# An explicit order of steps between first stage and out-projection, a mask inside VectorE's maximum, and adaLN sums twice as wide

## The chip, the cores and the metric

The kernel runs on one core of one Trainium2 chip. The core's engines work side by side, each in its own order of instructions: TensorE (PE: matmuls; PEld: its weight loads), VectorE (DVE), ScalarE (ACT), GpSimd (POOL), and SyncE (SP), which issues most DMAs. They wait for one another by semaphores. The metric is the device time of one execution in microseconds, as the median of several runs.

## What is computed

One layer of a hybrid decoder on 512 tokens of width 1024, in f32:

```python
mod = silu(c) @ w_ada + b_ada                  # sh1, sc1, gt1, sh2, sc2, gt2
h = rmsnorm(x) * (1 + sc1) + sh1
z = h @ w_in                                   # HGRN2: hq hf hi hg; NSA: nq, 6 x kv, gates
o_hg = rmsnorm(hgrn2(hq, hf, hi)) * silu(hg)   # 4 heads of 128
o_nsa = g0 * compressed + g1 * selected + g2 * window    # 8 heads of 64, softmax each
x = x + gt1 * (concat(o_hg, o_nsa) @ w_out)
h2 = rmsnorm(x) * (1 + sc2) + sh2
a, v = split(causal_dwconv(h2 @ w_up))
x = x + gt2 * ((silu(a) * v) @ w_down)
```

With 512 tokens, 8 blocks of 64 and 16 to be selected, the selected branch is plain causal attention over all blocks, and the window of 512 also covers every earlier token. So both branches are causal attention with keys and values of their own.

## The kernel before

**Stages.** The tokens lie in four tiles of 128. Every f32 product of the projections is done as three matmuls of split operands (`mm3`, L143 to L146: high by high, high by low, low by high); `split` (L139) makes the parts, the high one by a cast on ACT (L140), the low one by a subtraction on DVE (L141). First come the adaLN sums for the first norm, the norm and the query and forget projections of the first stage (to about 60 us). Then, until 289 us, the section that the change concerns: the remaining input projections, HGRN2 and the attention, all mixed. Then the output projection (`oh`), the up-projection (`u`) to 590 us, and the down-projection (`dn`) to the end.

**The section's streams.** It is made of Python generators, each of which issues some instructions and yields:

- the dense chain: key/value projection (`kva`), a second one, the HGRN2 query, forget, value and gate projections (`pT`: six matmuls of 512 columns per step), the compression of blocks (`cmp_hidden`) and, at its end, the rest that comes ahead of the output projection (`late`);
- `prep`: norm and rotation of queries and keys. `hrs` is the reciprocal root (POOL, L367), `xr` the scaled row (DVE, L703), `dst` the rotated one (L710, L712), `qhl` its split; PE transposes that (L769, `ps`);
- `hg_levels(0)` and `hg_levels(1)`: HGRN2 by levels of doubling block length, with products `lev` on PE (L1138) and masks, decays and states (`hgA`, `hgQ`, `hgK`, `hgtot`, `hgS`) mostly on DVE;
- `ada_sums`: the adaLN products for the later stages, as sums on DVE over tiles of w_ada: `aacc = aw * cs + aacc` (L1287, the first of a row by L1289), 512 columns at a time;
- `attention`: one unit after another.

**An attention unit** is one head of one tile of queries. For tiles 0 and 1 it does both branches at once (n = 2); for tiles 2 and 3 each branch (b) is a unit of its own (n = 1), 32 in all; a further unit per tile is the compressed branch. A unit goes through stations that are staggered over the units: `scores` (two matmuls into a PSUM bank `S`, L984 and L985; a third with the identity adds the causal mask to the diagonal block, L986; DVE takes the negated maximum, L988), `expo` (ACT, L1005: exponential from `S` into `pt`, with the row sum), `weigh` (at every odd head, for the pair: reciprocal and gate on DVE, L1019 and L1020; then both heads' `pt` are scaled, by DVE for b = 0, L1027, by ACT for b = 1, L1025), `flip` (PE transposes `pt` into bank `F`, L1036; ACT copies it, L1043), and `values` (matmuls with `pT`). `LAG = 4`: a unit's flip is issued four units after its scores.

**What sets the order.** Each engine executes its instructions in the order in which the program issues them. `emit` mixes streams in proportion to a number given to each: the next step comes from the stream whose share done is smallest. The section is a series of such calls, with the shares AN, DN, L0N, L1N, KVN, AD0 to AD6 and ADN.

Of the kernel before, what the change touches and what calls it, by code (L numbers as in the profile page):

```python
# [39 lines left out]
FP1 = 4  # L40
FP3 = 6
LAG = 4
AN = 82
DN = 29
L1N = 40
L0N = 19
KVN = 16
PREP1 = ('sq2 sq3 rq2 rq3', '', 'nq0', 'fq0', 'nq1', '', 'lq0', 'fq1', 'nq2', '', 'lq1', 'fq2', 'nq3', 'lq2', 'fq3', 'lq3')
PREP2 = ('sk0 rk0 sk1 rk1', 'nk0 fk0 sk2 rk2', 'nk1 fk1 sk3 rk3', 'lk0 nk2 fk2')
PREP3 = ('lk1 nk3 fk3 sa0 ra0', 'sa1 ra1 lk2 na0 fa0', 'sa2 ra2 lk3 na1 fa1', 'sa3 ra3 la0 na2 fa2')  # L50
PREP4 = ('', 'la1 na3 fa3', '', 'la2', '', 'la3', '', '')
ROWS = (2, 3, 5)
COLS = (0, 0, 1, 1, 2, 1, 2, 2)
SUMS = {3: (4, 4, 4), 5: (6, 5, 3), 6: (7, 5, 3)}
# [2 lines left out]
VLAG = 1  # L57
ADL = 1
ADAS = (3, 4, 2)
ADW = 512  # L60
AD0, AD1, AD2, AD3, AD4, AD5, AD6 = 8, 4, 0, 0, 4, 4, 2
ADN = 26
LEVELS = (1, 2, 4, 8, 16, 32, 64)

C_IDENT = 0
# [34 lines left out]
def hybrid_layer_kernel(ctx: ExitStack, tc: tile.TileContext, d: dict, out: bass.AP, dbg=None):  # L100
# [21 lines left out]
    def PS(s="ps"):  # L122
        return psum.tile([P, 512], F32, tag="b", name=nm(s))

    def TMP(shape, dt=F32, tag="tmp"):
        n = 1
        for a in shape[1:]:
            n *= a
        if n > 256:
            return tp.tile(shape, dt, tag="t2", name=nm(tag), bufs=8)  # L130
        return tp.tile(shape, dt, tag="t1", name=nm(tag), bufs=4)

    def SM(shape, tag, dt=F32):
        return sm.tile(shape, dt, tag=tag, name=nm(tag))
# [13 lines left out]
    def dump(name, ap):  # L148
        if dbg is not None:
            o = nc.dram_tensor("dbg_" + name, ap.shape, F32, kind="ExternalOutput").ap()  # L150
            sp.dma_start(o, f32(ap))
            dbg.append(name)

    def emit(*streams):

        st = [[0, max(n, 1), g] for g, n in streams]
        while st:
            e = min(st, key=lambda e: e[0] / e[1])
            e[0] += 1
            try:  # L160
                next(e[2])
            except StopIteration:
                st.remove(e)

    def chain(*gens):
        for g in gens:
# [710 lines left out]
    def cmp_flat():  # L877
        ps = PS()
        pe.transpose(ps[:, 0:32], perow, ident[0:32, 0:32])
        ve.tensor_copy(pet, ps[:, 0:32])  # L880
        for b in range(2):
            f = G([16, 2, 32], s="flat")
            gp.memset(f[:, :, :, 31:32], 0.0)
            for g in range(2):
                for m2 in range(2):
                    src = kv2[:, b, g, 8 * m2:8 * m2 + 248].rearrange("p (n m) -> p m n", m=8)
                    (gp if g else ve).tensor_tensor(f[:, 8 * m2:8 * m2 + 8, g, 0:31], src,
                                                    pet[:, b * 16 + 8 * m2:b * 16 + 8 * m2 + 8].unsqueeze(2)
                                                    .to_broadcast([P, 8, 31]), ALU.add)
# [86 lines left out]
    def scores(u):  # L976
        i, h, bs = u
        if h is None:
            return cmp_scores(i)
        g, W, n = h // 4, (i + 1) * P, len(bs)  # L980
        ps = PS("S")
        o = ps[:, 0:n * W].rearrange("p (b j t) -> p j b t", b=n, t=P)
        bsl = slice(bs[0], bs[0] + n)
        pe.matmul(o, QS[i][:, h], KK[g, 0][:, 0:i + 1, bsl], start=True, stop=False)  # L984
        pe.matmul(o, QS[i][:, h], KK[g, 1][:, 0:i + 1, bsl], start=False, stop=False)  # L985
        pe.matmul(o[:, i], identb, causb.unsqueeze(1).to_broadcast([P, n, P]), start=False, stop=True)  # L986
        mx = SM([P, 2], "mx")
        ve.tensor_reduce(mx[:, 0:n], ps[:, 0:n * W].rearrange("p (b w) -> p b w", b=n), AX.X, ALU.max,  # L988
                         negate=True)
        return ps, mx  # L990

    def expo(u, st):
        i, h, bs = u
        if h is None:
            sc.activation(st, st, AF.Exp)
            return st
        ps, mx = st
        W, n = (i + 1) * P, len(bs)
        pt = TMP([P, 512], tag="pt")
        if h % 2 == 0:  # L1000
            sums[0] = SM([P, 2, 2], "su")
        su = sums[0]
        for e in range(n):
            sl = slice(e * W, (e + 1) * W)
            sc.activation(pt[:, sl], ps[:, sl], AF.Exp, bias=mx[:, e:e + 1], accum_out=su[:, h % 2, e:e + 1])  # L1005
        return pt, su

    def weigh(u, st):
        i, h, bs = u
        if h is None:  # L1010
            cmp_norm(i, st)
            return st
        if h % 2 == 0:
            first[0] = st[0]
            return st[0]
        pt, su = st
        W, n = (i + 1) * P, len(bs)
        gv = gates[:, i].rearrange("p (h b) -> p h b", b=3)
        ve.reciprocal(su[:, :, 0:n], su[:, :, 0:n])  # L1019
        ve.tensor_tensor(su[:, :, 0:n], su[:, :, 0:n], gv[:, h - 1:h + 1, 1 + bs[0]:1 + bs[0] + n], ALU.mult)  # L1020
        for a, p_ in enumerate((first[0], pt)):
            for e, b in enumerate(bs):
                sl = slice(e * W, (e + 1) * W)
                if b:
                    sc.activation(p_[:, sl], p_[:, sl], AF.Copy, scale=su[:, a, e:e + 1])  # L1025
                else:
                    ve.tensor_scalar(p_[:, sl], p_[:, sl], su[:, a, e:e + 1], None, ALU.mult)  # L1027
        return pt
# [251 lines left out]
    def ada_sums():  # L1280
        for n, (s, k) in enumerate(ada_rows):
            if k == 0:
                aacc[s] = G([D], s="aacc")
            for c in range(0, D, ADW):
                o, w = aacc[s][:, c:c + ADW], aws[n][:, c:c + ADW]
                if k:
                    ve.scalar_tensor_tensor(o, w, cs[:, k:k + 1], o, ALU.mult, ALU.add)  # L1287
                else:
                    ve.tensor_scalar(o, w, cs[:, 0:1], None, ALU.mult)  # L1289
                if c + ADW == D and k == KT - 1:  # L1290
                    summed.append(s)
                yield
                if c + ADW == D:
                    ada_load()
# [28 lines left out]
    def ada_out():  # L1323
        for s in ADAS:
# [72 lines left out]
    gt1 = G([D], s="gt1")  # L1397
    sp.dma_start(gt1, d["b_ada"][0, 2 * D:3 * D].partition_broadcast(P))
    adas = ada_out()
    adss = ada_sums()  # L1400

    def late():
        for _ in range(4):
# [4 lines left out]
    def part(g, n):  # L1408
        for _ in range(n):
            if next(g, g) is g:  # L1410
                return
            yield

    gp.tensor_copy(causb, cb[:, C_CAUS:C_CAUS + P])
    kv = proj_kv()
    for _ in prep(("sq0 sq1 rq0 rq1",)):
        pass
    for j in range(2):
        hg_forget(0, j, accf[j])
    for _ in range(2):  # L1420
        ada_load()
    emit((kv, KVN), (prep(PREP1), len(PREP1)), (part(adss, AD0), AD0))
    emit((proj_a(), 8), (prep(PREP2), len(PREP2)), (part(adss, AD1), AD1))
    attn = attention(adas)
    lev0 = hg_levels(0, As[0])
    lev1 = hg_levels(1, As[1])
    emit((proj_T(lambda j, a: hg_query(0, j, a)), 8), (prep(PREP3), len(PREP3)), (part(adss, AD2), AD2))
    emit((proj_T(lambda j, a: hg_forget(1, j, a)), 8), (prep(PREP4), len(PREP4)), (part(attn, 10), 10), (part(adss, AD3), AD3))
    cmp_flat()
    hq1 = proj_T(lambda j, a: hg_query(1, j, a))  # L1430
    hv0 = proj_tok(hg_value_out)
    emit((chain(part(hq1, 4), cmp_hidden(0), cmp_hidden(1), hq1), 12), (part(attn, 12), 12),
         (part(lev0, 10), 10), (part(adss, AD4), AD4))
    emit((chain(part(hv0, 4), cmp_hidden(2), cmp_hidden(3)), 8), (part(attn, 6), 6), (part(lev0, 6), 6), (part(adss, AD5), AD5))
    dense = chain(hv0, hg_value_odd(), proj_T(hg_gate_out(0)), proj_T(hg_gate_out(1), False), late())
    emit((cmp_out(), 4), (part(dense, 4), 4), (part(attn, 4), 4), (part(lev0, 4), 4), (part(adss, AD6), AD6))
    emit((attn, AN), (dense, DN), (lev0, L0N), (lev1, L1N), (adss, ADN))
    assert len(summed) == 3
    for _ in adas:
        pass  # L1440
# [251 lines left out]
```

## Time and profile before

| | |
|---|---|
| Median of three runs | 716.05 us (714.89 to 716.3) |
| The profiled execution | 714.7 us; its span 712.9 us |
| Granted TensorE clock, mean | 1.00 |
| Busy | PE 98%, DVE 65%, ACT 45%, POOL 15% |
| The section: first kv matmul to first matmul ahead of the output projection | 60.2 to 289.3 us |

The span runs from the first to the last recorded instruction. A row of the timeline has the start in us, the duration in us, engine, line, operation, output<-input and shapes, how many instructions it stands for, and in brackets how long the engine had been idle just before and what released it. A row of grouped instructions ends with count, busy time in us, mean of one in ns, and idle time before them with its releasers. Durations of neighbours can overlap, since an engine takes up the next instruction while the last one drains; the distance from start to start is then the better price of one.

### The profile page before, as it was taken

Reading aid. Unit: us, or ns where it says so; the run is one execution under the profiler, and the core shown is the slowest. Engines: PE = TensorE matmul, PEld = TensorE weight load, DVE = VectorE, ACT = ScalarE, POOL = GpSimd, SP = SyncE. Lnnn points to the kernel's source line nnn. Section 1 sums busy time; section 2 is a strip of 40 time slices with the busy share of each in tenths; the row PEclk is TensorE's granted clock in tenths of the full one; section 3 lists DMA queues with packets and bytes.
Section 4 is the critical chain, followed back from the end, with each engine's and each line's share of the span. In section 5 each row is a group of like instructions: output and inputs, shape, how many; then the busy total and the mean of one; then the engine's idle time right before and its main releaser. Section 6 shows DMA issues by size and latency. Waiting matters only on the chain.

```text
span 712.9 us, 10152 instructions
## 1 busy us (share of the span) xinstructions
PE 700.6 (98%) x3912; PEld 575.9 (81%) x3912; DVE 462.7 (65%) x874; ACT 323.7 (45%) x618; POOL 108.0 (15%) x99
## 2 busy tenths in 40 slices
PE   8999999999999999999999999999999999999998
PEld 4767898788877878888998888888888888888886
DVE  5688797877988988878845656655555554224224
ACT  6555446555566577344643444345334433211210
POOL 1005021200000000110017717621110101000000
PEclk9999999999999999999999999999999999999999
DMA  9997453356323213514236336343243232225311
GB/s 289 292 275 222 122 177 114 96 159 224 119 61 119 60 60 119 178 60 123 60 90 177 108 100 174 121 119 109 68 119 104 74 119 83 94 88 178 103 46 60
DMA packets 100485, 90.20 MB, mean 127 GB/s; under 512 B 5787, under 2 KB 83411, under 8 KB 100437
## 3 DMA queue, kind: packets, MB, share of 16 engines
q1 hardware_dynamic: 100181, 89.44, 41.3%
q8 instruction: 31, 0.51, 0.3%
q10 hardware_dynamic: 256, 0.11, 0.1%
q14 instruction: 17, 0.14, 0.1%
HBM read 87.43 MB, written 2.11 MB: 126 GB/s over the span
## 4 chain that ended last, share of the span: by engine, by line
PE 72%; DVE 18%; ACT 4%; DMA 2%; SPq 2%; issue 1%; POOL 1%; ACTq 0%; POOLq 0%; DVEq 0%
PE u L145 11%; PE u L146 11%; PE u L144 11%; PE dn L145 6%; PE dn L146 6%; PE dn L144 6%; DVE mx L988 2%; DVE aacc L1287 2%; DVE wlo L141 1%; PE oh L144 1%; PE oh L146 1%; PE oh L145 1%; DVE rows L409 1%; PE pT L144 1%; PE pT L146 1%; PE pT L145 1%
## 5 line engine op out<-in xcount | busy, mean ns | idle before, releaser
L141 DVE TENSOR_TENSOR wlo<-raw,whi 128x1024 fp32r<-128x1024 f32 (+1 forms) x87 | 111.6, 1283 | 137.5 <-ACT whi L140 136.9
L144 PE MATMUL u<-h2h,whi 128*128 128x512 f32 (+1 forms) x360 | 136.8, 380 | 0.0
L145 PE MATMUL u<-h2l,whi 128*128 128x512 f32 (+1 forms) x360 | 136.8, 380 | 0.0
L146 PE MATMUL u<-h2h,wlo 128*128 128x512 f32 (+1 forms) x360 | 136.8, 380 | 0.0
L140 ACT CAST whi<-raw 128x1024 fp32r<-128x1024 f32 (+1 forms) x87 | 89.7, 1031 | 92.8 <-PE dn L146 80.1
L144 PEld LDWEIGHTS u<-h2h,whi 128*128 128x128 f32 x360 | 67.7, 188 | 12.8
L146 PEld LDWEIGHTS u<-h2h,wlo 128*128 128x128 f32 x360 | 67.7, 188 | 12.7
L145 PEld LDWEIGHTS u<-h2l,whi 128*128 128x128 f32 x360 | 67.7, 188 | 12.7
L145 PE MATMUL dn<-wlo,gT 128*128 128x512 f32 (+1 forms) x160 | 62.1, 388 | 0.0
L146 PE MATMUL dn<-whi,gT 128*128 128x512 f32 (+1 forms) x160 | 62.1, 388 | 0.0
L144 PE MATMUL dn<-whi,gT 128*128 128x512 f32 (+1 forms) x160 | 62.1, 388 | 0.0
L1579 POOL TENSOR_TENSOR y<-y,y 128x512 f32<-128x512 f32 x22 | 28.3, 1287 | 165.5 <-DVE y L1574 161.8
L367 POOL TENSOR_TENSOR hrs<-hrs,mhalf 128x4 f32<-128x4 f32 (+2 forms) x16 | 18.3, 1164 | 217.2 <-DVE hrs L366 217.2
L1005 ACT ACTIVATE pt<-S,mx 128x128 f32<-128x128 f32 (+3 forms) x64 | 33.7, 531 | 29.4 <-DVE mx L988 26.7
L140 ACT CAST gT<-y 128x512 fp32r<-128x512 f32 x20 | 12.4, 621 | 70.9 <-POOL y L1579 70.9
L141 DVE TENSOR_TENSOR gT<-y,gT 128x512 fp32r<-128x512 f32 x20 | 15.3, 767 | 42.6 <-ACT gT L140 42.6
L144 PE MATMUL pT<-hT,whi 128*128 128x512 f32 x96 | 41.3, 430 | 0.0
L146 PE MATMUL pT<-hT,wlo 128*128 128x512 f32 x96 | 37.8, 394 | 0.0
L145 PE MATMUL pT<-hT,whi 128*128 128x512 f32 x96 | 37.6, 391 | 0.0
L1577 ACT ACTIVATE y<-y 128x512 f32<-128x512 f32 x22 | 13.9, 632 | 50.1 <-DVE y L1574 50.1
L145 PEld LDWEIGHTS dn<-wlo,gT 128*128 128x128 f32 x160 | 30.1, 188 | 6.4 <-DVE wlo L141 0.2
L144 PEld LDWEIGHTS dn<-whi,gT 128*128 128x128 f32 x160 | 30.1, 188 | 6.2
(366 smaller groups left out, 1454.5 us busy)
## 6 DMA issues: line engine op xcount, KB each, us to landing
raw<-in_w_up SPq DMA_DIRECT2D x44, 512.0 KB, 5.1
aw<-in_w_ada SPq DMA_DIRECT2D x24, 512.0 KB, 3.9
raw<-in_w_down SPq DMA_DIRECT2D x10, 1024.0 KB, 5.2
ada<-in_w_ada SPq DMA_DIRECT2D x32, 256.0 KB, 5.4
raw<-in_w_in SPq DMA_DIRECT2D x7, 1024.0 KB, 5.0
x<-in_x SPq DMA_DIRECT2D x8, 512.0 KB, 5.6
raw<-in_w_cmp SPq DMA_DIRECT2D x8, 512.0 KB
raw<-in_w_out SPq DMA_DIRECT2D x4, 1024.0 KB, 5.9
```

The costliest lines, as they stand in the source:

```text
L140: sc.copy(hi, src)
L141: (eng or ve).tensor_tensor(lo, src, f32(hi), ALU.subtract)
L144: pe.matmul(o, ah, bh, start=start, stop=False, skip_group_check=True)
L145: pe.matmul(o, ah, bl, start=False, stop=False, skip_group_check=True)
L146: pe.matmul(o, al, bh, start=False, stop=stop, skip_group_check=True)
L367: gp.tensor_tensor(o, o, mhalf[:, 0:n], ALU.pow)
L409: ve.scalar_tensor_tensor(t, w, cs[:, j:j + 1], t, ALU.mult, ALU.add)
L988: ve.tensor_reduce(mx[:, 0:n], ps[:, 0:n * W].rearrange("p (b w) -> p b w", b=n), AX.X, ALU.max, negate=True)
L1005: sc.activation(pt[:, sl], ps[:, sl], AF.Exp, bias=mx[:, e:e + 1], accum_out=su[:, h % 2, e:e + 1])
L1287: ve.scalar_tensor_tensor(o, w, cs[:, k:k + 1], o, ALU.mult, ALU.add)
L1577: sc.activation(y, y, AF.Silu)
L1579: gp.tensor_tensor(ys[0], ys[0], y, ALU.mult)
```

## The change

Four things, and what goes with them:

1. `emit` and its shares are gone. One string of 353 letters names for each step the stream that it comes from: d dense chain, p prep, a attention, c compressed outputs, s adaLN sums, l and m the two pairs of HGRN2 levels. `cmp_flat` becomes a step of the dense chain.
2. In units with n = 1 the mask matmul is gone. DVE adds the mask and takes the maximum in one instruction, `tensor_tensor_reduce`: it writes -(S + mask) into `pt` in SBUF and the minimum of that into `mx`. The exponential then works in place on `pt`, with scale -1. The mask for it (`cmask`, bf16, 512 columns, the diagonal block last) is made by POOL at the start.
3. `ADW`, the width of the adaLN sums, goes from 512 to 1024: half as many instructions, twice as wide.
4. In tile 3 the odd head's scaling for b = 0 goes from DVE to ACT (four instructions).

```diff
-ADW = 512
-AD0, AD1, AD2, AD3, AD4, AD5, AD6 = 8, 4, 0, 0, 4, 4, 2
-ADN = 26
+ADW = 1024
+ORDER = ("ddpddsppdppddpppdpdpdspsppsdddpdddppdpdsdpddpdsdpdddpddddppddpaddappapaaaddpapddaappdpdddadadlalladl",
...
+         "aasdmaammsdsdamammdadaaalmamlaaamadladsamaaamdaladasd")
...
-    def emit(*streams):
...
-        pe.matmul(o, QS[i][:, h], KK[g, 1][:, 0:i + 1, bsl], start=False, stop=False)
+        pe.matmul(o, QS[i][:, h], KK[g, 1][:, 0:i + 1, bsl], start=False, stop=(n == 1))
+        mx = SM([P, 2], "mx")
+        if n == 1:
+            pt = TMP([P, 512], tag="pt")
+            ve.tensor_tensor_reduce(pt[:, 0:W], ps[:, 0:W], cmask[:, 512 - W:512], -1.0, 1e30, ALU.add, ALU.min,
+                                    mx[:, 0:1])
+            return pt, mx
         pe.matmul(o[:, i], identb, causb.unsqueeze(1).to_broadcast([P, n, P]), start=False, stop=True)
-        mx = SM([P, 2], "mx")
...
-        pt = TMP([P, 512], tag="pt")
+        pt = ps if n == 1 else TMP([P, 512], tag="pt")
...
-            sc.activation(pt[:, sl], ps[:, sl], AF.Exp, bias=mx[:, e:e + 1], accum_out=su[:, h % 2, e:e + 1])
+            sc.activation(pt[:, sl], ps[:, sl], AF.Exp, bias=mx[:, e:e + 1], scale=(-1.0 if n == 1 else 1.0),
+                          accum_out=su[:, h % 2, e:e + 1])
...
-                if b:
+                if b or (i == 3 and a):
                     sc.activation(p_[:, sl], p_[:, sl], AF.Copy, scale=su[:, a, e:e + 1])
...
     gp.tensor_copy(causb, cb[:, C_CAUS:C_CAUS + P])
-    kv = proj_kv()
+    gp.memset(cmask[:, 0:384], 0.0)
+    gp.tensor_copy(cmask[:, 384:512], cb[:, C_CAUS:C_CAUS + P])
...
-    emit((kv, KVN), (prep(PREP1), len(PREP1)), (part(adss, AD0), AD0))
...
-    emit((attn, AN), (dense, DN), (lev0, L0N), (lev1, L1N), (adss, ADN))
...
+    for row in ORDER:
+        for step in row:
+            next(streams[step], None)
```

The line numbers of the changed kernel are 7 to 14 lower in this part (L984 becomes L971, L1036 becomes L1029).

Three places where the instructions stand differently. The first is VectorE at the first HGRN2 levels, about 136 to 139 us before. `hgA` takes the products `lev` (masked), `hgQ` multiplies the query by a decay; `mx` are maxima of attention units, `aacc` the adaLN sums. Before:

```order
L988 TENSOR_REDUCE mx_1563<-S_1559 128x2
L1287 SCALAR_TENSOR_TENSOR aacc_767<-aw_736,cs,aacc_767 128x512
L1120 TENSOR_TENSOR hgA_1565<-lev_1566,cb 128x512
L988 TENSOR_REDUCE mx_1602<-S_1598 128x2
L1120 TENSOR_TENSOR hgA_1565<-lev_1587,cb 128x512
L1122 TENSOR_TENSOR hgQ_1268<-hgQ_1268,hgT_726 128x1024
```

And now, on the same engine at the same step:

```order
L1020 TENSOR_SCALAR pt_1482<-pt_1482,su_1422 128x128
L980 TENSOR_REDUCE mx_1565<-S_1562 128x2
L1113 TENSOR_TENSOR hgA_1574<-lev_1575,cb 128x512
L1113 TENSOR_TENSOR hgA_1574<-lev_1588,cb 128x512
L1115 TENSOR_TENSOR hgQ_1236<-hgQ_1236,hgT_729 128x1024
```

No sum and no second maximum stands between the `hgA` and ahead of `hgQ`.

The second place is TensorE at the first two units of the last tile (`qs_970` before, `qs_969` now, are its queries; `S` a score, `F` the transposes of a unit four places earlier, `pT` with `hT` a projection). Before:

```order
L984 MATMUL S_2770<-KK_1060,qs_970 128x512
L985 MATMUL S_2770<-KK_1061,qs_970 128x512
L986 LDWEIGHTS identb
L986 MATMUL S_2770<-causb,identb 128x128
L1138 MATMUL lev_2776<-hgQ_1268,hgE_2565 128x2x64 x4
L1036 MATMUL F_2785<-cb,pt_2644 128x128 x3
L144 MATMUL pT_2678<-hT_509,whi_2519 128x512
L145 MATMUL pT_2678<-hT_509,whi_2519 128x512
L146 MATMUL pT_2678<-hT_509,wlo_2520 128x512
L144 MATMUL pT_2678<-hT_561,whi_2519 128x512
L145 MATMUL pT_2678<-hT_561,whi_2519 128x512
L146 MATMUL pT_2678<-hT_561,wlo_2520 128x512
```

Now, on TensorE from the same unit on:

```order
L971 MATMUL S_2742<-KK_1059,qs_969 128x512
L972 MATMUL S_2742<-KK_1060,qs_969 128x512
L1029 MATMUL F_2748<-cb,pt_2608 128x128 x3
L971 MATMUL S_2760<-KK_1059,qs_969 128x512
L972 MATMUL S_2760<-KK_1060,qs_969 128x512
L1029 MATMUL F_2766<-cb,pt_2642 128x128 x3
L141 MATMUL pT_2694<-hT_509,whi_2498 128x512
L142 MATMUL pT_2694<-hT_509,whi_2498 128x512
L143 MATMUL pT_2694<-hT_509,wlo_2499 128x512
L141 MATMUL pT_2694<-hT_561,whi_2498 128x512
```

The mask matmul and its weight load are gone, and two units follow each other with no projection and no level between them.

The third place is the end of the section on VectorE, from the last sum ahead of the compressed branch's normalisation (`csu`) to `wol`, the low part of the output projection's weights; `hgS` are HGRN2's states. Before (two more pairs of `hgS` rows and a third sum stand between the last row here and `wol`):

```order
L1287 SCALAR_TENSOR_TENSOR aacc_2657<-aw_736,cs,aacc_2657 128x512
L970 TENSOR_REDUCE csu_3308<-sc_636_3267 128x8
L971 RECIPROCAL csu_3308<-csu_3308 128x8
L973 SCALAR_TENSOR_TENSOR csu_3308<-csu_3308,cb,gates 128x8
L974 TENSOR_TENSOR sc_636_3267<-sc_636_3267,csu_3308 128x256
L1178 COPY hgS_3246<-lev_3247 128x128
L1180 SCALAR_TENSOR_TENSOR hgS_3246<-hgS_3246,hgtot_2920,lev_3247 128x128 x2
L1287 SCALAR_TENSOR_TENSOR aacc_2657<-aw_736,cs,aacc_2657 128x512
```

Now, on VectorE, from the last state ahead of the normalisation's product to `wol`:

```order
L961 TENSOR_TENSOR sc_634_3211<-sc_634_3211,csu_3268 128x256
L1171 COPY hgS_3234<-lev_3235 128x128
L1173 SCALAR_TENSOR_TENSOR hgS_3234<-hgS_3234,hgtot_3131,lev_3235 128x128 x2
L1171 COPY hgS_3217<-lev_3242 128x128
L1173 SCALAR_TENSOR_TENSOR hgS_3217<-hgS_3217,hgtot_2857,lev_3242 128x128 x2
L1280 SCALAR_TENSOR_TENSOR aacc_2542<-aw_739,cs,aacc_2542 128x1024
L1171 COPY hgS_3234<-lev_3276 128x128
L1173 SCALAR_TENSOR_TENSOR hgS_3234<-hgS_3234,hgtot_3131,lev_3276 128x128 x2
L138 TENSOR_TENSOR wol_3324<-raw_2695,woh_3323 128x1024
```

One sum of 1024 columns is left where three of 512 were.

More of the change, by code (lines that the diff above doesn't have):

```diff
@@ L42 @@
 LAG = 4
[L43 to L51, printed above, removed]
+PREP = ('sq2 sq3 rq2 rq3', '', 'nq0', 'fq0', 'nq1', '', 'lq0', 'fq1', 'nq2', '', 'lq1', 'fq2', 'nq3', 'lq2', 'fq3',
+        'lq3', 'sk0 rk0 sk1 rk1', 'nk0 fk0 sk2 rk2', 'nk1 fk1 sk3 rk3', 'lk0 nk2 fk2', 'lk1 nk3 fk3 sa0 ra0',
+        'sa1 ra1 lk2 na0 fa0', 'sa2 ra2 lk3 na1 fa1', 'sa3 ra3 la0 na2 fa2', '', 'la1 na3 fa3', '', 'la2', '', 'la3',
+        '', '')
 ROWS = (2, 3, 5)
@@ L59 @@
 ADAS = (3, 4, 2)
-ADW = 512
-AD0, AD1, AD2, AD3, AD4, AD5, AD6 = 8, 4, 0, 0, 4, 4, 2
-ADN = 26
+ADW = 1024
+ORDER = ("ddpddsppdppddpppdpdpdspsppsdddpdddppdpdsdpddpdsdpdddpddddppddpaddappapaaaddpapddaappdpdddadadlalladl",
+         "aaaldsdaldladasdadaadsladladllsldadadlldlsdadladlcdcasaalcsslacddalalmmmadddaaadmsaaaammaaadallmaaaa",
+         "ladalmdmaamaddmmldaamsamsaaaldaadlmdaasmaamaamdlammdaaaadladalasdamalammdaadaamammlamasdalamlalaaamd",
+         "aasdmaammsdsdamammdadaaalmamlaaamadladsamaaamdaladasd")
 LEVELS = (1, 2, 4, 8, 16, 32, 64)
@@ L152, in dump @@
             dbg.append(name)
-    def emit(*streams):
[L156 to L163, printed above, removed]
     def chain(*gens):
@@ L891, in cmp_flat @@
         cps.append(PS("cps"))
+        yield
     def cmp_hidden(mq):
@@ L1331, in ada_out @@
                 yield
+    cmask = cst.tile([P, 512], BF16, name="cmask")
     adr = hbm.tile([2, D], F32, name="adr")
@@ L1399, in hybrid_layer_kernel @@
     adas = ada_out()
-    adss = ada_sums()
     def late():
@@ L1421, in hybrid_layer_kernel @@
         ada_load()
-    emit((kv, KVN), (prep(PREP1), len(PREP1)), (part(adss, AD0), AD0))
[L1423 to L1429, printed above, removed]
     hq1 = proj_T(lambda j, a: hg_query(1, j, a))
     hv0 = proj_tok(hg_value_out)
[L1432 to L1436, printed above, removed]
-    emit((attn, AN), (dense, DN), (lev0, L0N), (lev1, L1N), (adss, ADN))
+    dense = chain(proj_kv(), proj_a(), proj_T(lambda j, a: hg_query(0, j, a)),
+                  proj_T(lambda j, a: hg_forget(1, j, a)), cmp_flat(), part(hq1, 4), cmp_hidden(0), cmp_hidden(1),
+                  hq1, part(hv0, 4), cmp_hidden(2), cmp_hidden(3), hv0, hg_value_odd(), proj_T(hg_gate_out(0)),
+                  proj_T(hg_gate_out(1), False), late())
+    streams = {"d": dense, "p": prep(PREP), "a": attention(adas), "c": cmp_out(), "s": ada_sums(),
+               "l": hg_levels(0, As[0]), "m": hg_levels(1, As[1])}
+    for row in ORDER:
+        for step in row:
+            next(streams[step], None)
+    for g in streams.values():
+        assert next(g, g) is g
     assert len(summed) == 3
```

## Prediction, written before the changed kernel was run

> **What bounds the kernel now.** I read the page first, then the busy time of each engine by stretch, then PE's own waits, and only then single instructions around each wait.
>
> ```profile
> span 712.9 us, 10152 instructions
> PE 700.6 (98%) x3912; PEld 575.9 (81%) x3912; DVE 462.7 (65%) x874; ACT 323.7 (45%) x618; POOL 108.0 (15%) x99
> ```
>
> PE is recorded as busy for 98% of the span. The table by stretch (length, then each engine's busy time, clock last but two) shows where the other 2% is:
>
> ```profile
> 60.20:120.00 59.80, 59.16 (x336) 51.27 (x335) 51.22 (x132) 27.27 (x60) 13.25 (x13) 1.00 0.43 133
> 120.00:150.00 30.00, 29.05 (x176) 21.89 (x175) 24.86 (x53) 19.51 (x67) 4.03 (x5) 1.00 0.55 176
> ...
> 200.00:232.00 32.00, 30.39 (x225) 24.39 (x224) 26.15 (x59) 20.92 (x50) 0.00 (x0) 1.00 0.30 98
> 232.00:270.00 38.00, 37.60 (x279) 29.61 (x279) 33.48 (x77) 25.07 (x58) 0.00 (x0) 1.00 0.19 56
> ...
> 347.00:590.00 243.00, 243.00 (x1148) 204.42 (x1146) 142.68 (x172) 105.33 (x150) 74.93 (x56) 1.00 0.38 109
> ```
>
> The clock is 1.00 throughout, and from 347 to 590 us PE never stops, so nothing there can give. The edited part runs from the first kv matmul at 60.2 us to the output projection at 290. In the stretches shown PE idles for 0.64 + 0.95 + 1.61 + 0.40 = 3.6 us (the two left out between 150 and 289 us have no idle), over half of it in 200 to 270 us, the attention. DVE is busy for 82 to 88% there, so its queue is the one that decides. PE's longest waits by name (total, times, longest):
>
> ```profile
> PE F L1036 <- ACT pt L1025: 1.1, 3, 0.6
> PE oh L145 <- DVE wol L141: 1.1, 1, 1.1
> ...
> PE F L1036 <- DVE pt L1027: 0.7, 1, 0.7
> ```
>
> The wait for wol comes just behind the section: 3.6 + 1.1 = 4.7 us in all, of which these rows are 2.9 and two single waits shown below, 0.78 and 0.64, another 1.4. So the kernel is the tight sum of PE's instructions plus less than 5 us of waits, and a gain can come from those two only: fewer PE nanoseconds, or fewer waits.
>
> **The change, part by part: PE's own work.** The mask matmul (L986) leaves 32 units. Its record is 0.23 us long, but what it costs is the distance to the next start:
>
> ```profile
> 204.89 0.23 PE L986 MATMUL S<-causb,identb 128*128 128x128 bf16 x1
> 204.93 0.47 PE L144 MATMUL pT<-hT,whi 128*128 128x512 f32 x1
> 205.24 0.39 PE L145 MATMUL pT<-hT,whi 128*128 128x512 f32 x1
> 205.47 0.40 PE L146 MATMUL pT<-hT,wlo 128*128 128x512 f32 x1
> ...
> 207.86 0.23 PE L986 MATMUL S<-causb,identb 128*128 128x128 bf16 x1
> 207.92 1.13 PE L1138 MATMUL lev<-hgQ,hgE 128*128 128x128 f32 x8
> ```
>
> That is 0.04 us ahead of a projection and 0.06 ahead of the small matmuls. I take 0.055: 32 x 0.055 = 1.75 us, all on the path (1.3 to 1.9 by the two rows). The same rows give the price of a changeover: the first projection matmul behind other work holds PE for 0.31 us, the next for 0.23, so 0.08 each time. Between kv and the output projection the explicit order has 48 runs of projection matmuls where the old one has 57: 9 x 0.08 = 0.7 us. Together 2.45 us (2.0 to 2.6) that no wait can hide, unless it comes back as a wait.
>
> **DVE's work.** Its rows, by shape, in 60 to 290 us:
>
> ```profile
> L1287 DVE SCALAR_TENSOR_TENSOR aacc<-aw,cs,aacc 128x512 f32<-128x512 f32 x42 | 31.1, 746 | 0.0
> ...
> L1005 ACT ACTIVATION_READ_ACCUMULATOR pt<-S,mx 128x1 f32 x64 | 12.9, 202 | 0.0
> ...
> L1005 ACT ACTIVATE pt<-S,mx 128x512 f32<-128x512 f32 x16 | 11.1, 693 | 10.8 <-DVE mx L988 9.3 <-DVE su L1019 1.5
> ...
> L988 DVE TENSOR_REDUCE mx<-S 128x1 f32<-128x512 f32 x16 | 10.9, 685 | 1.2 <-PE S L986 1.2
> ...
> L1025 ACT ACTIVATE pt<-pt,su 128x512 f32<-128x512 f32 x8 | 5.3, 712 | 0.0
> ...
> L1027 DVE TENSOR_SCALAR pt<-pt,su 128x512 f32<-128x512 f32 x8 | 3.5, 484 | 0.1
> ...
> L1019 DVE RECIPROCAL su<-su 128x2 f32<-128x2 f32 x16 | 2.5, 158 | 1.4 <-ACT pt L1005 1.4
> ```
>
> The 42 sums of 512 columns become 21 of 1024. That width is in no row for this operation; the nearest is a two-input wlo of the same width, 1.23 us (a row of it follows below), and two narrow ones would be 1.49. I take 1.28: 42 x 0.746 - 21 x 1.28 = 4.4 us less. Four scalings go to ACT: 4 x 0.484 = 1.9 less here, 4 x 0.712 = 2.8 more there, where ACT is busy about two thirds of the time. The new maximum reads as much as the old one (0.685 at 512) and a second instruction fetches the result. That one is in no row: between ACT's fetch of the same kind (0.202) and nothing; I take DVE's own smallest, the reciprocal, 0.158. 32 x 0.16 = 5 us more (0 to 6.5). DVE's sum is then 1.3 us lower, between 0.2 more and 6.3 less. So the edits hardly relieve DVE as a whole; they move its load.
>
> The Trainium skill (VectorE: DVE Perf Modes, The TRN2 errata) has a fixed 58 cycles plus one per element for an instruction on SBUF operands, which would make the fetch about 61 ns (an estimate) and the 32 of them 2 us. By that DVE's sum would fall by 4.3 us instead of 1.3, and the same section's own remark, that the fixed part measures nearer 150 cycles, fits the 158 ns row. I keep the row.
>
> **The waits.** First, the start (VectorE's xr, waited for by the transposes at L769). DVE's stretch and PE's first transposes behind it:
>
> ```profile
> 68.92 1.23 DVE L141 TENSOR_TENSOR wlo<-raw,whi 128x1024 fp32r<-128x1024 f32 x1 [0.26 <-ACT whi L140]
> 70.06 0.69 DVE L703 TENSOR_TENSOR xr<-accq,hrs 128x512 f32<-128x512 f32 x1
> ...
> 70.90 0.53 PE L769 MATMUL ps<-identr,qhl 128*128 128x128 f32 x3 [0.64 <-DVE xr L703]
> ```
>
> The bank that they write becomes free with that xr. In the new order wlo goes ahead of qhl, so that neither waits long for ACT (0.26 us in this row for wlo, about as much for qhl), and the sum between is gone (about 0.4), while the one ahead of the first xr gets wider (0.25 to 0.3 more). xr comes 0.5 to 0.8 us sooner, against a wait of 0.64: gone or 0.1 left. POOL's added memset and cast stand ahead of its hrs powers:
>
> ```profile
> 58.80 0.29 POOL L1414 CAST causb<-cb 128x128 bf16<-128x128 f32 x1
> 59.06 3.33 POOL L367 TENSOR_TENSOR hrs<-hrs,mhalf 128x8 f32<-128x8 f32 x2
> ```
>
> By the cast's row the two take about 0.3 us each (the memset is twice as wide, so up to 0.9 in all). The powers end at 62.4, and the xr above, which uses the second, starts at 70.06: hidden by that distance; without it, 0.9 once.
>
> Second, the first levels (lev waits for hgQ):
>
> ```profile
> 136.42 0.73 DVE L1287 SCALAR_TENSOR_TENSOR aacc<-aw,cs,aacc 128x512 f32<-128x512 f32 x1
> ...
> 137.68 0.41 DVE L988 TENSOR_REDUCE mx<-S 128x2 f32<-128x256 f32 x1
> ...
> 138.15 0.44 PE L1036 MATMUL F<-cb,pt 128*128 128x128 f32 x2
> 138.35 0.48 PE L984 MATMUL S<-KK,qs 128*128 128x512 f32 x1
> 138.66 0.40 PE L985 MATMUL S<-KK,qs 128*128 128x512 f32 x1
> 138.90 0.28 PE L986 MATMUL S<-causb,identb 128*128 128x256 bf16 x1
> 139.96 0.35 PE L1138 MATMUL lev<-hgQ,hgE 128*128 128x128 f32 x1 [0.78 <-DVE hgQ L1122]
> ```
>
> The sum (0.73) and the second maximum (0.41) no longer stand ahead of hgQ. Neighbours on DVE overlap by some 0.09 (in the fence below, a sum of 0.75 is followed after 0.66), so hgQ comes 1.14 - 0.18 = 0.96 us sooner against 0.78. Gone. The last two rows also show that a stop costs more than its record: from start to start 1.06 us pass where a mask matmul takes about 0.05, so 1.0 is lost, 0.2 beyond the 0.78.
>
> Third, the end of the section (oh waits for wol):
>
> ```profile
> 289.77 0.75 DVE L1287 SCALAR_TENSOR_TENSOR aacc<-aw,cs,aacc 128x512 f32<-128x512 f32 x1
> 290.43 2.35 DVE L141 TENSOR_TENSOR wol<-raw,woh 128x1024 fp32r<-128x1024 f32 x2
> ...
> 291.71 0.50 PE L145 MATMUL oh<-wol,mixN 128*128 128x512 f32 x1 [1.10 <-DVE wol L141]
> ```
>
> Behind the last compressed scores DVE has three narrow sums (about 2 us by start to start) before wol, in the new order one wide one (1.28): 0.7 to 0.9 us sooner. 0.3 of the 1.10 is left; if DVE arrives late there, as after two wide sums shortly before, up to 1.1.
>
> Fourth, the attention of the last two tiles, 2.0 us of idle (1.61 + 0.40). Here the order is built differently: units with no projection between them stand in pairs (score, three transposes, score, three transposes), and longer projection runs follow. Each F still comes four units after its score. By the rows at 138 us a score costs PE 0.31 + 0.24 and a transpose 0.1, so a pair is 2 x (0.55 + 0.3) = 1.7 us of PE work. DVE has two maxima of 0.69 + 0.16 in it and, at the start of the last tile, the compressed branch's normalisation, which takes 1.3 us from its first row to what follows it:
>
> ```profile
> 283.95 0.41 DVE L970 TENSOR_REDUCE csu<-sc 128x8 f32<-128x256 f32 x1
> ...
> 285.24 0.29 DVE L1178 COPY hgS<-lev 128x128 f32<-128x128 f32 x1
> ```
>
> That is 3.0 us. DVE falls behind by 1.3 there, and by up to 2.8 with the small instructions and sums that the new order puts around it, counted unit by unit with such rows; the projection run after it gives that back. In the old order the same count falls behind by at most 2.1 us, in the stretch from 200 to 232 that has 1.61 us of idle. So I expect about the same kind of waits in fewer places: 1.1 us of the 2.0 left. The bank of a score is freed by DVE's maximum now, not by ACT's exponential, and the exponential in place reads SBUF; both cost PE nothing while no score waits for a bank, and no such wait is in PE's list above.
>
> **The sum**, against the profiled run (714.7 us, span 712.9 and 1.8 around it): -2.45 of PE work; -0.6 at the start, -0.8 at the levels, -0.8 at the end, -0.9 in the attention; -0.6 for what four stops cost beyond their records. Together -6.2: 708.5. The median of the runs, 716.05, lies 1.35 above the profiled one, so the forecast is **709.8 us**.
>
> **Rivals.** *All waits go.* 2.6 + 4.7 + 1.4 (seven stops at 0.2) = 8.7: 706.0, on the median's scale 707.3. For it: DVE has 12 to 18% of its time free in the attention. Against: the pairs above. Chance 0.08, at 707.5 and below.
>
> *The waits only move.* PE's 2.45 us are saved, the sum of waits stays near 4.7: 712.3, or 713.6. For it: DVE's load falls by 1.3 us only, and the tight pairs ask more of it at once. Against: two of the waits removed are tied to one instruction in DVE's queue, and the count shows that instruction earlier. Chance 0.15 (712.5 to 714.6). If new waits also eat the 2.45 us, nothing changes within 0.2% (1.4 us, about what a measurement of this kernel can tell from no change): 0.10.
>
> *Slower: the pairs starve PE.* The mechanism is DVE's queue at six places in the attention (around the compressed normalisation, and where wide sums stand between maxima). By the same count as above DVE is behind at them by 1.5, 1.7, 2.3, 2.8, 1.2 and 1.4 us, 10.9 in all. If each appears as a wait of the F's four units on, the time is 714.7 - 2.45 - 4.7 + 10.9 = 718.4, or 719.8. It decides at the lead: from a score to its F the new order has about 6 to 8 us of PE work, the bare chain (maximum 0.85, exponential 0.9, reciprocal and product 0.3, two scalings 1.2) takes 3.2, so a delay of 2.8 just fits into 6. A fetch above 0.2 us, or wide sums near 1.5, takes that margin. Chance 0.12. That the dropped mask matmul was free, hidden beside other work, would only lower 2.45 to 0.7 and stays inside the first two cases.
>
> **How the numbers follow.** The forecast's own case (707.5 to 712.5) has 0.55; with the rivals, faster 0.55 + 0.08 + 0.15 = 0.78, same 0.10, slower 0.12. The range 706.8 to 715.2 leaves out the slower case, half of the unchanged one and a sliver at the bottom.
>
> **What would show it.** In the new profile: no L986 row for 128x128; no PE wait for xr at 70 us and none for hgQ; oh's wait for wol under 0.5; F's waits, now for pt from either engine, near 1 us in 200 to 270 and at the starts of pairs. The fetch's row near 0.16 and the wide sum near 1.28 carry DVE's sum. It is wrong if PE's idle time between 60 and 297 us is above 4 us, if the fetch is over 0.2, or if the wide sum costs two narrow ones.

## The result and the profile after

The changed kernel takes 704.54 us (median of 4 runs, 704.15 to 705.5) against 716.17 us for the kernel before on the same chip (714.89 to 716.4, 4 runs). The ratio is 0.984, with a 95% interval of 0.983 to 0.986: faster by 11.6 us. The forecast said 709.8, and its range ended at 706.8, so the sign was right and the gain nearly twice as large as forecast (6.3). The profiled execution took 704.15 us. One run of all those below, of the kernel before with the sooner weighing, took 772.75 us at a granted clock of 0.85 and is left out.

The page's first lines of the changed kernel, with the span 10.6 us shorter:

```profile
span 702.3 us, 10102 instructions
PE 693.7 (99%) x3879; PEld 577.8 (82%) x3880; DVE 457.7 (65%) x878; ACT 327.5 (47%) x622; POOL 109.2 (16%) x101
```

Busy time by stretch in the changed kernel, in the columns of the prediction's table. The section now runs from 60.43 to 280.23 us:

```profile
60.40:111.00 50.60, 50.60 (x289) 44.55 (x288) 43.44 (x102) 23.34 (x47) 13.14 (x10) 1.00 0.50 158
111.00:150.00 39.00, 39.00 (x239) 31.44 (x238) 34.62 (x82) 26.43 (x88) 5.58 (x8) 1.00 0.47 150
150.00:198.00 48.00, 48.00 (x415) 42.49 (x414) 40.13 (x92) 26.82 (x68) 0.00 (x0) 1.00 0.53 164
198.00:200.00 2.00, 1.36 (x10) 1.06 (x9) 2.00 (x3) 1.92 (x4) 0.00 (x0) 1.00 0.01 4
200.00:232.00 32.00, 32.00 (x241) 27.10 (x240) 28.10 (x76) 21.71 (x52) 0.00 (x0) 1.00 0.24 83
232.00:262.00 30.00, 30.00 (x222) 25.66 (x222) 25.50 (x69) 23.94 (x53) 0.00 (x0) 1.00 0.12 36
262.00:280.20 18.20, 18.20 (x186) 16.48 (x183) 15.54 (x41) 13.73 (x28) 0.00 (x0) 1.00 0.41 136
280.20:288.00 7.80, 7.80 (x50) 6.75 (x50) 6.16 (x13) 2.71 (x5) 1.09 (x2) 1.00 0.92 359
```

PE idles for 0.64 us in the whole section, in one place, and not at all behind it; before it was 3.6 and 1.1. DVE is about as busy in the attention as it was (85 to 88% of the time, 82 to 88% before): its work got less, and so did the time for it. What its relief was worth, the experiments show.

From the first kv matmul to the first `hgo` matmul, the section took 289.32 - 60.18 = 229.14 us and takes 280.23 - 60.43 = 219.80: 9.3 of the 10.6 us. The stage behind it gives 1.5 (the wait for `wol`), and the head of the program differs by 0.25 the other way, which varies like that from run to run (the first kv matmul starts at 60.2 to 61.3 us in the profiled runs of this study). Of the 9.3 us, 4.6 are PE's stops: summed as time from start to start above the usual for the pair of instructions, they were 5.5 us at eleven places and are 0.9 at one. The other 4.7 us are PE's instructions themselves, where 2.45 had been forecast.

The start of the section in the changed kernel: DVE's second `xr`, and PE behind it.

```profile
68.86 0.68 DVE L138 TENSOR_TENSOR qhl<-dst,qhl 128x512 fp32r<-128x512 f32 x1
69.47 0.68 DVE L689 TENSOR_TENSOR xr<-accq,hrs 128x512 f32<-128x512 f32 x1
...
69.95 1.00 PE L755 MATMUL ps<-identr,qhl 128*128 128x128 f32 x8
```

`xr` starts 0.59 us sooner than before (70.06), and all eight transposes are one row with no gap. The end of the section:

```profile
277.41 1.28 DVE L1280 SCALAR_TENSOR_TENSOR aacc<-aw,cs,aacc 128x1024 f32<-128x1024 f32 x1
...
279.57 2.36 DVE L138 TENSOR_TENSOR wol<-raw,woh 128x1024 fp32r<-128x1024 f32 x2
...
281.36 0.40 PE L142 MATMUL oh<-wol,mixN 128*128 128x512 f32 x1
```

The first of the two `wol` is done at about 280.8 (half of that row), ahead of its use at 281.36, and PE doesn't wait for it. The one wait that is left, around 199 us:

```profile
198.30 1.31 DVE L1140 COPY_PREDICATED hgA<-cb,lev 128x512 f32<-128x512 uint8 x1
...
198.44 0.60 PE L1200 MATMUL ps<-cb,hvT 128*128 128x128 f32 x4
199.67 0.50 PE L141 MATMUL pT<-hT,whi 128*128 128x512 f32 x1 [0.64 <-DVE hgA L1140]
```

A projection waits for `hgA`, presumably as the last reader of the PSUM bank that it writes: no wait of a kind that the kernel before had.

The new and changed operations, grouped by shape:

```profile
L1280 DVE SCALAR_TENSOR_TENSOR aacc<-aw,cs,aacc 128x1024 f32<-128x1024 f32 x21 | 26.9, 1281 | 0.1
...
L997 ACT ACTIVATE pt<-pt,mx 128x512 f32<-128x512 f32 x16 | 11.7, 730 | 3.3 <-DVE mx L976 3.3
L976 DVE CUSTOM_DVE_ANT_0 pt<-S,cmask 128x512 f32<-128x512 f32 x16 | 10.8, 687 | 2.4 <-PE S L972 2.4
...
L976 DVE DVE_READ_ACCUMULATOR2_ANT mx<- 128x1 f32 x32 | 2.7, 86 | 0.0
```

The wide sum costs what was assumed (1.28), the maximum with the mask no more than the old one (687 against 685 ns). The fetch is 86 ns long, and even that is not what it costs:

```profile
195.67 0.55 DVE L976 CUSTOM_DVE_ANT_0 pt<-S,cmask 128x384 f32<-128x384 f32 x1
196.15 0.08 DVE L976 DVE_READ_ACCUMULATOR2_ANT mx<- 128x1 f32 x1
196.15 0.16 DVE L1012 RECIPROCAL su<-su 128x2 f32<-128x2 f32 x1
```

The next instruction starts with it, and so it does behind all 25 fetches where DVE didn't wait. From start to start the maximum and its fetch take 0.48 us, where the old maximum of this width took 0.47.

### The profile page after: what moved, and what is told of

The parts are those of the page before. It is cut to its first block, busy times and chain, and to the rows that moved or that the text cites. A ratio compares the mean times of both kernels' runs of the same rounds, so it can differ in the third digit from the quotient of the medians.

```text
span 702.3 us, 10102 instructions
## 1 busy us (share of the span) xinstructions
PE 693.7 (99%) x3879; PEld 577.8 (82%) x3880; DVE 457.7 (65%) x878; ACT 327.5 (47%) x622; POOL 109.2 (16%) x101
## 4 chain that ended last, share of the span: by engine, by line
PE 85%; DVE 8%; DMA 3%; SPq 2%; ACT 1%; issue 1%; POOL 0%; ACTq 0%; POOLq 0%; DVEq 0%
PE u L141 11%; PE u L143 11%; PE u L142 11%; PE dn L142 6%; PE dn L143 6%; PE dn L141 6%; PE pT L141 3%; PE pT L143 3%; PE pT L142 3%; PE oT L1057 2%; PE F L1029 2%; PE oh L141 2%; PE oh L143 2%; PE oh L142 2%; PE lev L1131 1%; DVE rows L395 1%
## 5 line engine op out<-in xcount | busy, mean ns | idle before, releaser
L141 PE MATMUL pT<-hT,whi 128*128 128x512 f32 x96 | 39.7, 414 | 0.6 <-DVE hgA L1140 0.6
L142 PE MATMUL pT<-hT,whi 128*128 128x512 f32 x96 | 37.5, 391 | 0.0
L141 PEld LDWEIGHTS dn<-whi,gT 128*128 128x128 f32 x160 | 30.0, 188 | 6.2
L143 PEld LDWEIGHTS dn<-whi,gT 128*128 128x128 f32 x160 | 30.0, 188 | 6.0
```

Source lines behind the costliest of these rows:

```text
L141: pe.matmul(o, ah, bh, start=start, stop=False, skip_group_check=True)
L142: pe.matmul(o, ah, bl, start=False, stop=False, skip_group_check=True)
L143: pe.matmul(o, al, bh, start=False, stop=stop, skip_group_check=True)
```

## The experiments

The numbers below are medians of several runs, each against runs of the kernel before made in the same session; differences of less than about 1 us between two of them are told from the length of the section in one profile each (229.14 us before, 219.80 in the changed kernel). The kernel before had a median of 716.2 us beside the changed kernel and of 715.2 to 715.5 in these later sessions, so the gain of the whole change is 11.6 by the one and about 10.8 by the others, and gains of different sessions compare to about 1 us only.

**The order alone.** Everything else is as before; where the order has a wide sum, two narrow ones are issued.

```diff
-ADW = 1024
+ADW = 512
...
-        if n == 1:
-            ve.tensor_tensor_reduce(...)
...
         pe.matmul(o[:, i], identb, causb...)
...
-                if b or (i == 3 and a):
+                if b:
```

> The new order with everything else as before: mask matmul back, narrow sums (two of 512 in each step where the order has one of 1024), tile 3's scalings back on DVE. Theory P (the order itself takes the waits away and starts projections at fewer places): PE's 6 us of lost time at waits go, and about 9 of the 19 slow projection starts; 7 to 8.5 us below before. Theory D (the waits went because the mask and the wide sums relieved DVE): 3 to 5 us of waits come back, mostly F for pt, and only 2 to 4 us below before.

707.73 against 715.18 us: 7.5 below (ratio 0.989, 0.988 to 0.991). The section takes 222.6 us, and PE's list of waits has no entry between 60 and 297 us. So the order takes the waits away by itself; the mask and the wide sums are not needed for that.

**All but the order.** The old streams with the new mask, the wide sums (and so half the shares for them) and the moved scalings.

```diff
-AD0, AD1, AD2, AD3, AD4, AD5, AD6 = 8, 4, 0, 0, 4, 4, 2
-ADN = 26
+AD0, AD1, AD2, AD3, AD4, AD5, AD6 = 4, 2, 0, 0, 2, 2, 1
+ADN = 13
```

> The old order with the new mask, the wide sums (shares of the sums halved) and the moved scalings. Theory P: only PE's own saving for the mask, 32 x 0.06 = 1.9 and up to 0.7 for 8 projection starts behind a score: 2 to 3 us below before, and PE's idle time stays at 4 to 5. Theory D: the waits at 70, 139 and 290 us and those of F go here too: 5 to 8 us below.

715.03 against 715.18: nothing (ratio 0.9997, 0.9988 to 1.0006). Both theories expected a gain, and both were wrong. PE's waits have grown by about what its instructions had shrunk: 3.2 us at F for pt from ACT (1.1 before), 1.3 for hgQ (0.8 before).

**The mask alone in the old order, and all but the mask in the new one.** The two edits are those of the change, in one kernel and taken back in the other.

> The kernel before with the new mask only. Theory P: PE's 1.9 to 2.7 us are saved, but the waits for DVE stand at fixed points of DVE's queue, and some of it turns into longer waits: 1 to 2.7 us below before. Theory D: less wait as well: 4 us below.

715.49 against 715.18: nothing either (0.9995 to 1.0013). PE's waits in this kernel:

```profile
PE F L1042 <- ACT pt L1031: 3.9, 4, 1.4
PE oh L145 <- DVE wol L141: 1.3, 1, 1.3
PE F L1042 <- DVE pt L1033: 1.0, 2, 0.8
```

F's waits were 1.1 and 0.7 before, and are 3.9 and 1.0: 3.1 us more. The section is as long as before (229.27). PE arrives sooner and waits at the same spots for a chain on DVE and ACT that got no shorter: from a pair's odd score to its scaled rows it takes 8.5 us on average before and 8.8 here, and the first F that waits in the attention comes 146.9 us behind the first kv matmul before and 147.0 here.

> The changed kernel with the mask matmul and the plain maximum back in all units. Theory P: PE's own cost of the mask comes back, 1.9 us by start to start plus 0.085 for each of about 10 projection runs that start behind a score: 2.7 us above the changed kernel, with no new waits. Theory D: DVE's maximum and fetch cost what they did, ACT's exponential reads PSUM again; waits of 1 us and more at F come back: 4 us or more above.

706.61 against 715.18: 8.6 below, against 11.6 for the whole change. The section takes 222.0 us, 2.2 more than with the new mask, and there is no new wait. The mask is worth 2 to 3 us in the new order and nothing in the old.

**The mask matmul put back beside the new maximum**, for PE's price of it alone. The mask is then added twice, which changes no weight.

```diff
         if n == 1:
+            pe.matmul(o[:, i], identb, causb.unsqueeze(1).to_broadcast([P, n, P]), start=False, stop=True)
             pt = TMP([P, 512], tag="pt")
```

> The changed kernel with the mask matmul issued as well (the mask is added twice, so the softmax is the same), DVE unchanged: PE's price of it alone. By the prediction's rows, 32 x 0.055 = 1.75 us above the changed kernel. By the theory that a projection behind a mask matmul also starts slowly, where one right behind a 512 or 384 wide score matmul doesn't: 10 slow starts more (23 to 33) at 0.09, so 2.7 us; 0.9 of it may hide the one wait left at 199 us.

706.33 against 715.5: 9.2 below, about 2 above the changed kernel; the section grows by 2.3. By start to start, the mask matmuls take 1.86 us, the projections 0.80 more, and the wait at 199 us is 0.5 shorter: 2.2. One place of the changed kernel, a score followed by a projection:

```profile
206.34 0.34 PE L972 MATMUL S<-KK,qs 128*128 128x384 f32 x1
206.52 0.39 PE L141 MATMUL pT<-hT,whi 128*128 128x512 f32 x1
206.75 0.40 PE L142 MATMUL pT<-hT,whi 128*128 128x512 f32 x1
```

And the same place with the mask matmul back:

```profile
207.24 0.34 PE L972 MATMUL S<-KK,qs 128*128 128x384 f32 x1
207.42 0.23 PE L975 MATMUL S<-causb,identb 128*128 128x128 bf16 x1
207.46 0.47 PE L141 MATMUL pT<-hT,whi 128*128 128x512 f32 x1
207.77 0.40 PE L142 MATMUL pT<-hT,whi 128*128 128x512 f32 x1
```

The matmul holds PE for 0.04 us, and the projection behind it for 0.31 where it was 0.23. Slow starts of `pT` projections (over 0.29 us to the next start) number 42 before, 23 in the changed kernel, 33 in this one.

**Narrow sums in the new order**, two per step:

```diff
-ADW = 1024
+ADW = 512
...
-                yield
                 if c + ADW == D:
+                    yield
                     ada_load()
```

> The changed kernel with the sums in steps of 512 again, two in each step, so that they stand where the wide one stood. Theory P (the order's places decide; the fetch of the maximum costs almost nothing): a pair of narrow sums takes DVE 1.32 us from start to start where the wide one takes 1.2, and the places are the same, so 0 to 1 us above the changed kernel. Theory D (DVE's relief by 4 us is what took the waits away): 2 to 4 us above, as waits at F.

705.32 against 715.5: 10.2 below. The section takes 220.8 us, 1.0 more; the longest new stop is 0.4 us (from start to start) at an F at 232.2 us. The relief of DVE by wide sums is worth about 1 us, not 2 to 4.

**Tile 3's scalings back on DVE** (`if b:`).

> The changed kernel with the four scalings of tile 3 back on DVE. Both theories: DVE has 1.9 us more over the tile, ACT 2.8 less; the slack at the pairs of tile 3 is 0.15 to 2.3 us, so at most one F wait of some 0.3 appears: 0 to 0.5 us above the changed kernel.

705.17 against 715.24: 10.1 below. The section takes 220.6 us, 0.8 more, of which 0.67 (0.5 in PE's list of waits) is one F wait at 256.5 us.

**One small DVE instruction more behind each new maximum:**

```diff
+            ve.tensor_copy(mx[:, 1:2], cs[:, 0:1])
             return pt, mx
```

> The changed kernel with one more small DVE instruction (a copy of one column into an unused one) behind each of the 32 new maxima: what a fetch of about 0.2 us would have done. By the slower rival of the prediction, DVE falls behind by four units' delay, 0.4 to 0.8 us, in each of the six tight places, and F waits there: 2 to 5 us above the changed kernel. By the theory that the order leaves DVE time at most places, with slack under 0.7 us at seven of sixteen pairs: 0.5 to 2 us above.

704.91 against 715.5: 10.6 below; the section takes 220.6 us, 0.8 more. The copy is 0.15 us long, but from start to start it costs less than half of that:

```profile
196.51 0.08 DVE L976 DVE_READ_ACCUMULATOR2_ANT mx<- 128x1 f32 x1
196.51 0.15 DVE L978 COPY mx<-cs 128x1 f32<-128x1 f32 x1
196.57 0.16 DVE L1013 RECIPROCAL su<-su 128x2 f32<-128x2 f32 x1
```

Behind the 25 copies where DVE didn't wait the next instruction came after 0.066 us, so all 32 add 2.1 us to DVE, and not the 0.2 us each that this run was meant to try. With that much more, the pairs of units don't starve PE: F waits at one place, for 0.19 us. The mechanism of the slower rival isn't there at this size; a delay of 0.2 us a unit was not tried.

**Two edits of the order at the wait that is left.** The first puts one step of the second pair's levels two places earlier (letters `llm` become `mll`), the second puts the projection half a unit later (`da` becomes `ad`).

> The changed kernel with one step of the second pair's levels two places earlier in the order, so that hgA's copy, which frees the bank that the projection at 199 us waits for, stands ahead of the other pair's four instructions. If that wait is DVE's queue and nothing else: the 0.9 us go, 0.5 to 0.9 below the changed kernel, with no new wait over 0.3. If it only moves, the same time, with the wait at the lev or F behind it.

704.76 against 715.5 (10.7 below); section 219.6. The wait is still there, at 0.8 us instead of 0.88: `hgA` of the other pair is now the last of DVE's four, and what the projection waits for comes about as late.

> The changed kernel with the projection that waits at 199 us one half step later, so that the next unit's transposes stand ahead of it. The bank that it writes is freed no earlier, but PE has 0.3 us of other work before it, and the run behind it is one piece where it was cut: 0.3 to 0.6 us below the changed kernel; if the F put first waits itself, no gain.

705.27 against 715.24 (10.0 below); section 220.6. The wait only moved to the transposes ahead of the projection. Neither beats the changed kernel.

**One unit more of lead in the old order**, `LAG = 5`, without and with the new mask.

> The kernel before with LAG = 5: a unit's transposes come five units after its scores, all else as it was. Theory L (in the old order the way from an odd score to its scaled rows takes 9 to 11 us at the pairs where PE waits, because a projection run stands between that unit and the next one, behind which its weighing is queued; the lead of four units is just as long): with one unit more of lead the F waits go, 2 to 3.5 us below before. Rival B (the eight temporary buffers that the units share become the limit): the same time or slower.

715.04 against 715.24: nothing (0.9988 to 1.0006). PE's longest waits between 60 and 297 us in this kernel:

```profile
PE lev L1138 <- DVE hgQ L1122: 1.3, 1, 1.3
PE ps L1207 <- ACT hvT L1198: 0.9, 1, 0.9
PE S L984 <- DVE hgA L1147: 0.8, 1, 0.8
PE oT L1049 <- ACT pT L1043: 0.8, 1, 0.8
```

The F waits for `pt` are gone, as expected, but waits for other products of DVE and ACT have taken their place: a longer lead removes these waits and gains no time.

> The old order with the new mask and LAG = 5. Theory L: the mask's PE saving (2.6 us), which went into longer F waits at LAG = 4, shows now, together with the F waits that go: 4 to 6 us below before. Rival B: pt is now held from the maximum on, longer than before, and the shared buffers stall DVE: less than 1 us below before, or slower.

716.04 against 715.24: 0.8 above (1.0004 to 1.0022). Here the mask's saving goes into such waits too.

**The dense steps spread evenly**, from the 170th step on, in the new order; all other steps keep theirs.

> The changed kernel with the dense steps of the attention's second half (from the 170th step on) spread evenly among the other steps, whose own order stays. If the exact places of the dense steps are what takes the waits away (each gives DVE time where its queue is long): 2 to 5 us above the changed kernel, as waits at F and at banks. If the order of the DVE-heavy steps among themselves does it (units, levels, sums): under 1 us above.

708.38 against 715.25: 6.9 below, about 4 less than the changed kernel. The section takes 223.5 us, 3.7 more. PE's waits:

```profile
PE oT L1054 <- ACT pT L1033: 1.2, 1, 1.2
PE F L1026 <- ACT pt L994: 1.0, 1, 1.0
PE F L1026 <- DVE sc L958: 0.7, 1, 0.7
PE ps L1197 <- ACT hvT L1188: 0.6, 1, 0.6
```

At 15 of the 16 pairs of heads in the last two tiles, the even head's F now comes 1.5 us or more after its rows are scaled (in the changed kernel it is under 0.7 at seven of the 16). The waits stand at 187 and 201 us and at 274 and 283 us, at the two ends of this half, and there are 28 slow starts instead of 23; that the even spread leaves too little projection work there is the likely reason, not a tested one. So the places of the dense steps are worth about 4 us against an even spread, and the tight pairs of units cost nothing.

**A unit's weighing half a step sooner**, in the old order and in the new.

```diff
-            if 0 <= s - 1 < n:
-                st[s - 1] = weigh(us[s - 1], st[s - 1])
             yield
+            if s < n:
+                st[s] = weigh(us[s], st[s])
```

> The kernel before with each unit's weighing issued half a step sooner, right ahead of the next unit's scores and not behind what follows them. If the old order's F waits come from the weighing's late place in DVE's queue: the way from odd score to scaled rows gets 1 to 3 us shorter, F waits go, 1.5 to 3.5 us below before. If the waits only change their name, as with one unit more of lead: within 1 us of before; slower by up to 3 if DVE now stands waiting for ACT's exponential.

718.49 against 715.25: 3.2 slower (ratio 1.0041 to 1.0067). The first half of the expectation came true: the way from the odd score to the scaled rows takes 7.4 us on average instead of 8.5, and F no longer waits for `pt`. But PE waits longer elsewhere. These two waits were 1.1 and 0.8 us:

```profile
PE oh L145 <- DVE wol L141: 2.2, 1, 2.2
PE lev L1138 <- DVE hgQ L1122: 2.1, 1, 2.1
```

At the first levels the weighing's reciprocal, product and two scalings now stand between the two `hgA` and so ahead of `hgQ` in DVE's queue (138.85 to 139.64 us), where before they came behind it. And in the attention DVE stands at the reciprocal for ACT's exponential, where that was 1.4 us:

```profile
DVE su L1019 <- ACT pt L1005: 3.7, 4, 2.2
```

So this edit too took F's waits out of the old order, and the time went into other waits for DVE.

> The changed kernel with the same sooner weighing. The places of its order were chosen with the later one, and PE has one wait of 0.9 us left: nothing to gain beyond that, so between 0.5 below and 2 above the changed kernel, above if DVE stands waiting for ACT.

713.19 against 715.25, 2.1 below: it gives back about 8.6 us of the change's gain, where 2 had been the expected limit. PE stops at many places again, for 1.1 us at most; the places of this order had been chosen with the later weighing.

## Why the prediction was right in sign and too small

The gap between forecast and measured time is 5.3 us. 1.0 us of it is only the scale: 1.35 us had been added to get from the profiled run to the median, and the changed kernel's median lies 0.4 above its profiled run. The rest, 10.6 us of span where 6.2 had been forecast, is about half in the waits and half in PE's own work.

**The waits: the count of the attention failed.** The start, the levels and the end went as worked out, and the end better: nothing of the 0.3 us was left. In the attention 1.1 of 2.0 us had been left standing, and no wait at F stayed, only 0.64 us of another kind. The step that failed is the count by which packed units put DVE behind and PE waits there: that DVE is behind by 1 to 3 us at a pair has no price as long as the lead covers it. It does: the lead from an odd score to the pair's first F is 8.8 us on average, and the chain with all its queueing takes 7.7 (the prediction had 6 to 8 us for the lead and 3.2 for the bare chain). The even spread, which takes the pairs apart and is slower, shows so; the small instruction added to each unit, at 0.066 us, fits it. From start to start the stops in the attention were 3.2 us at seven places, and the section's 5.5 us became 0.9. Together with the 1.4 at `oh` that is 6.0 us in place of the 3.7 forecast (3.1 of records and 0.6 beyond them). POOL's added instructions stayed hidden, as forecast (0.41 and 0.28 us; the memset is three times as wide as the cast, not twice).

**PE's work: the mechanism was right and the size was off.** The mask matmul was forecast at 1.75 us and measured at 1.86 to 1.9. The changeover, 9 x 0.08 = 0.7, was the term that was mis-sized: it counted runs of projections (57 to 48), as if each began slowly. A projection right behind a score without mask does not. 19 slow starts went (42 to 23), 1.6 us: nine by the order, as forecast (33 are left with the order alone), and ten because the mask matmul ahead of them is gone (33 again where it is put back). About 1.2 us more of PE's 4.7 lie in other changes of neighbours and weren't taken apart; this part stays open. This is also why the range ended too high: its lower end assumed that all waits go, and took PE's own saving as 2.6 at most.

**DVE's sum.** The fetch was taken as 0.16 us, and costs nothing from start to start. DVE's work fell by 6.1 us (42 narrow sums, 31.1 us, became 21 of 26.9; 1.9 us of scalings left), near the far end of the bounds (6.3). These are lengths of records, though, and so were the prediction's. From start to start a pair of narrow sums takes 1.32 us and the wide one 1.20, a scaling 0.40, and the new maximum 0.01 more than the old: about 4 us less. It mattered little: narrow sums cost 1.0 us, and scalings 0.8.

The estimate of 61 ns from the Trainium skill's figure for an instruction on SBUF operands (VectorE: DVE Perf Modes, The TRN2 errata) was nearer to the 86 ns of the record than the 158 ns row. Neither is the price in this queue, which is 0 from start to start.

**The rivals.** "All waits go" is what came, at 0.08 the least likely, and below its own time of 707.3, since PE saved more. "The waits only move" is wrong for the whole change. Its second case, that new waits also eat PE's saving, is what its parts did: the mask alone, and all but the order, gained nothing. The slower rival's mechanism was not there.

**What the order does.** It is worth 7.5 us alone; the rest is worth nothing alone, and about 3 us on top of it (2.8 by the length of the section). How long ACT waits for DVE in the attention changed too. ACT's two longest waits for DVE in the kernel before, 190 to 289 us:

```profile
ACT pt L1005 <- DVE mx L988: 18.9, 17, 3.1
ACT pt L1025 <- DVE su L1020: 5.5, 4, 2.1
```

And in the changed kernel, 186 to 280 us:

```profile
ACT pt L997 <- DVE mx L976: 14.5, 12, 3.0
...
ACT pt L1018 <- DVE su L1013: 2.6, 2, 1.4
```

24.4 us have become 17.1. But this sum doesn't tell the time of a kernel: it is 20.5 us with the order alone, which has no wait of PE, and 14.4 with the dense steps spread evenly, which is slower. The way from a pair's odd score to its scaled rows says more. It takes 8.5 us on average before and 7.7 after (at most 11.3 and 10.5), and the lead from that score to the pair's first F is 9.2 and 8.8. The order alone does this: 7.8 and 9.1 there. So the chain got shorter by more than the lead did. It isn't the whole account either, since the sooner weighing made the chain as short in the old order and the time went to other waits. The places of the dense steps are about 4 us of the order's gain, against an even spread; which of the other exchanges in the order give the rest wasn't tried one by one, and stays open.

## What to carry to other kernels

PE was 98% busy here and the rest was small waits for a chain on other engines, and taking instructions from PE gave nothing until the order of that chain had been changed: the mask's 2 to 3 us came only with it. In such a kernel, before a part is priced by its instructions, ask which wait of PE stands next behind it, and whether that wait hangs on PE's arrival or on another engine's. And price a matmul together with the start of what follows it.

## What the runs showed of the hardware

- DVE's fetch of a reduced value, 86 ns long, starts together with the next instruction (196.15 and 196.15 us): 0 from start to start, where a copy of one column is 149 ns long and takes 66 ns from start to start.
- The first 512-wide projection matmul holds PE for 0.31 us behind a 128-wide bf16 mask matmul and for 0.23 behind a 384-wide f32 score matmul, at the same place of the program.
- ACT's exponential takes 730 ns from SBUF and took 693 from PSUM (512 columns); PE has no wait for it in the changed kernel.
